# Layer norms of a two-layer trunk: sums over channels and their factors taken as whole tiles

## The chip, the cores and the metric

The kernel runs on one core of a Trainium2 chip. Times are device microseconds of one execution. A row of the profile has times in microseconds from the start of the profiled execution, and names a line of the kernel as L followed by its number. The engines are TensorE (PE; its weight loads are PEld), VectorE (DVE), ScalarE (ACT), GpSimd (POOL) and SyncE (SP), which issues most transfers.

## The reference

The input x has 1024 tokens with 1024 channels, in float32. Each layer computes x = x + mixer(rmsnorm(x)), and a last rmsnorm follows:

```python
def rmsnorm(x, g):
    xf = x.astype(jnp.float32)
    y = xf * lax.rsqrt(jnp.mean(xf * xf, axis=-1, keepdims=True) + EPS)
    return (y * g.astype(jnp.float32)).astype(x.dtype)
```

Layer 0 projects h to six parts (u, a gate, q, k, v, a second gate). u goes through a diagonal state-space recurrence and a GLU, q, k and v through retention in chunks of 64 tokens; each result is multiplied by its SiLU gate, and one product maps both back to 1024 channels. Layer 1 projects to a, b and g, convolves a * sigmoid(b) over 31 tokens per channel, norms the result over the channels with mean and variance, and applies SiLU, the gate and an output product:

```python
    mu = jnp.mean(uf, axis=-1, keepdims=True)
    var = jnp.mean(jnp.square(uf - mu), axis=-1, keepdims=True)
    uf = (uf - mu) * lax.rsqrt(var + EPS) * ln_g.astype(jnp.float32) + ln_b.astype(jnp.float32)
```

So there are four norms, each with a factor per token that is the inverse root of a mean over all channels.

## The kernel before

Activations lie with channels on the 128 partitions and tokens along the free dimension, so that a 1024 x 1024 activation is eight channel blocks of 128 x 1024, handled as two halves of 512 tokens. A product of 1024 channels with one 128-column weight block is 24 matmuls of 128 x 128 by 512: the operands are split into a high and a low part in the format fp32r, and each of the eight channel blocks takes three products, high by high, high by low and low by high (`mm3`, L181 to L183). SP streams the weight blocks of 512 KB from HBM through three buffers; ACT makes the high part (L171) and DVE or POOL the low part (L172). Products gather in PSUM banks: three for running products (`mm`), five for other uses in the front, two kinds for the convolution later.

Nobody writes the order of the instructions by hand. A scheduler places each instruction on its engine's queue as its operands allow, by a priority that `self.at(number)` sets (lower goes first), and `issue_after(x)` forbids an instruction to be placed ahead of x. What two instructions share on one engine they do in the queue's order: a waiting instruction holds those behind it.

A norm before the change goes in these steps. The squares of the eight channel blocks are added up to one tile, on ACT with DVE or POOL. `token_sums` (L444) sums that tile over the partitions: for each 128 tokens the data is the stationary operand and 64 columns of ones the moving one, so that the sum of a token lands on the token's own partition. `rsqrt` (L453, L454) then works on 4 or 8 values per partition: a square root on ACT and a reciprocal on DVE. To multiply the channel-major tiles, the factor must be on all partitions along the free dimension: `spread_split` makes diagonal tiles, the identity times the factor, a high and a low one, and multiplies ones by them (L473); `spread` (L483) does it with one f32 product per 256 columns.

The places are these.

- `layer0_front`: the tile R0 (`self.R`, all partitions, 1024 tokens) and `Rtok` (the same factors, tokens on partitions, which the retention's v blocks use). The first products are u blocks 0 and 1 for both halves; then u2 (the half 0 in one piece, half 1 in eight steps of three products), with the token sums behind step 0 and the spreads before step 5; ACT copies the spread factors from PSUM to R (L335). Then DVE evacuates the blocks: `u_block(nb)` multiplies the block's two PSUM banks by R into a tile `ut` (L356), which has two buffers, and SP stores that tile to `u_d`. Blocks 0, 1 and 2 are evacuated from banks that were filled before R; block 3 and later ones compute into a running bank, half by half, so that they need a bank which an earlier evacuation has freed. On DVE's queue beside the evacuations are steps on the parameters of the recurrence (lines L531 to L549) and low parts of weights.
- `h1(h)`, the norm ahead of layer 1, one factor for each half (r1). The eight blocks are then scaled by it (L1374) and split into high and low parts for the products b, g and a.
- `conv_norm(h)`, with two sums (values and squares), the variance and the factor on 4 values per partition, and two spreads: the factor (cR) and the mean times the factor (cD).
- `final_norm`: half 0 as a whole, half 1 in two quarters of 256 tokens. The last quarter ends the kernel; it keeps PE running with a few products that nobody reads (`idle`) and spreads twice, one copy for ACT (`rf_C`).

The products around a norm have `hold` lists: at which step of which block the product must stay behind the sums or spreads of the norm (`self.hold`, `among`, `norm_mm`), and one list of convolution steps on DVE that must stay behind a norm's diagonals (`NORM_TAPS`).

## Time and profile before

| | |
|---|---|
| median of 3 runs | 1183.63 us (1182.59 to 1185.37) |
| profiled execution | 1188.26 us, span 1186.5 us |
| PE | 1173.5 us busy, 99 % |
| PE weight loads | 985.8 us, 83 % |
| DVE | 851.1 us, 72 % |
| POOL | 657.4 us, 55 % |
| ACT | 483.6 us, 41 % |
| mean granted clock of PE | 0.995 of full speed |
| HBM traffic | 216 GB/s over the span |

The span is the time between the first and the last instruction of the profiled execution. A row of the timeline gives start and busy time, engine, line, operation, output<-inputs, the shape (for a matmul the stationary tile and then the moving one), and how many like instructions it joins; a bracket at the end gives the idle time before it and who ended it. A row of the waits gives an engine's instruction, the one that it waited for, the total of the waits, their number and the longest. A row of the windows gives the stretch, its length, the busy time and instructions of PE, PEld, DVE, ACT and POOL, the granted clock, the share of the DMA engines and GB/s.

### The profile page before, as it was taken

How to read it: one execution, taken by the hardware profiler on the slowest of the kernel's cores; microseconds unless marked ns; L12 is line 12 of the kernel's file. 1: busy time of each engine (PE TensorE's matmuls, PEld its weight loads, DVE VectorE, ACT ScalarE, POOL GpSimd, SP SyncE). 2: the span in 40 equal slices, each digit the busy share in tenths (PEclk: the TensorE clock that was granted, in tenths of full speed). 3: DMA queues.
4: the chain of work that ended last, by engine and by line, in shares of the span. 5: the costliest groups of instructions: out<-in, count | busy, mean ns of one | idle time of the engine just before them, and what ended most of it. 6: DMA issues, size and time to landing. Idle time of an engine off the chain costs nothing.

```text
span 1186.5 us, 17318 instructions
## 1 busy us (share of the span) xinstructions
PE 1173.5 (99%) x6326; PEld 985.8 (83%) x6326; DVE 851.1 (72%) x1479; ACT 483.6 (41%) x712; POOL 657.4 (55%) x448
## 2 busy tenths in 40 slices
PE   9999999999999999899999999999999999999997
PEld 7888888888888889889888888888888888888886
DVE  7975698777427458476679422699999999989743
ACT  6322232222222231333546322545435676434662
POOL 2059999888145354232574110678444567767753
PEclk9999999999999999999999999999999999999999
DMA  9344355565387676759998987655668754357874
GB/s 355 107 129 136 131 156 167 182 186 170 109 280 280 233 231 181 259 177 343 371 344 290 336 266 254 213 198 196 227 243 280 231 180 166 107 189 253 268 246 145
DMA packets 117637, 261.46 MB, mean 220 GB/s; under 512 B 10672, under 2 KB 42288, under 8 KB 116912
## 3 DMA queue, kind: packets, MB, share of 16 engines
q1 hardware_dynamic: 117552, 260.36, 65.4%
q8 instruction: 49, 0.80, 0.3%
q14 instruction: 36, 0.29, 0.1%
HBM read 181.48 MB, written 74.65 MB: 216 GB/s over the span
## 4 chain that ended last, share of the span: by engine, by line
PE 93%; DMA 3%; DVE 2%; issue 1%; SPq 0%; POOL 0%; ACT 0%; POOLq 0%; DVEq 0%; ACTq 0%
PE mm_g L181 8%; PE mm_g L183 7%; PE mm_g L182 7%; PE mm_wo L182 5%; PE mm_wo L181 5%; PE mm_wo L183 5%; PE mm_b L182 2%; PE mm_b L183 2%; PE mm_a L183 2%; PE mm_a L182 2%; PE mm_b L181 2%; PE mm_a L181 2%; PE mm_oc L181 2%; PE mm_oc L183 2%; PE mm_oc L182 2%; PE mm_u L183 2%
## 5 line engine op out<-in xcount | busy, mean ns | idle before, releaser
L1467 DVE SCALAR_TENSOR_TENSOR cv<-u,convw,cv 128x512 f32<-128x512 f32 x398 | 273.7, 751 | 9.0 <-ACT cv L1450 6.9
L1444 POOL TENSOR_TENSOR tp<-tp,tp 128x512 f32<-128x512 f32 x64 | 83.7, 1307 | 35.2 <-ACT tp L1443 34.0
L181 PE MATMUL mm_g<-xh,wh_g 128*128 128x512 f32 x256 | 101.8, 398 | 0.0
L183 PE MATMUL mm_g<-xh,wl_g 128*128 128x512 f32 x256 | 100.1, 391 | 0.0
L182 PE MATMUL mm_g<-xl,wh_g 128*128 128x512 f32 x256 | 100.0, 391 | 0.0
L415 POOL TENSOR_TENSOR s1q<-s1q,s1q 128x512 f32<-128x512 f32 x12 | 17.7, 1478 | 85.2 <-ACT s1q L410 85.2
L1443 ACT ACTIVATE tp<-u,convw 128x512 f32<-128x512 f32 x64 | 45.6, 719 | 37.3 <-POOL tp L1444 35.8
L181 PEld LDWEIGHTS mm_g<-xh,wh_g 128*128 128x128 f32 x256 | 48.0, 188 | 11.7 <-issue 1.2
L183 PEld LDWEIGHTS mm_g<-xh,wl_g 128*128 128x128 f32 x256 | 48.1, 188 | 10.4
L182 PEld LDWEIGHTS mm_g<-xl,wh_g 128*128 128x128 f32 x256 | 48.1, 188 | 9.9 <-issue 0.4
L371 DVE TENSOR_TENSOR gt<-mm_g,R 128x512 f32<-128x512 f32 x32 | 21.9, 684 | 46.5 <-PE mm_g L183 46.4
L172 POOL TENSOR_TENSOR wl_glu<-wf_glu,wh_glu 128x1024 fp32r<-128x1024 f32 x14 | 34.0, 2428 | 33.8 <-ACT wh_glu L171 33.2
L183 PE MATMUL mm_oc<-zh,wl_woc 128*128 128x512 f32 (+1 forms) x144 | 52.5, 366 | 0.0
L172 POOL TENSOR_TENSOR wl_v<-wf_v,wh_v 128x1024 fp32r<-128x1024 f32 x12 | 31.1, 2601 | 38.5 <-ACT wh_v L171 38.5
L182 PE MATMUL mm_oc<-zl,wh_woc 128*128 128x512 f32 (+1 forms) x144 | 52.5, 366 | 0.0
L181 PE MATMUL mm_oc<-zh,wh_woc 128*128 128x512 f32 (+1 forms) x144 | 52.3, 369 | 0.0
L181 PE MATMUL mm_g<-h1h,wh_cg 128*128 128x512 f32 x128 | 49.9, 390 | 0.0
L181 PE MATMUL mm_wo<-ysh,wh_wos 128*128 128x512 f32 x128 | 49.9, 390 | 0.0
L182 PE MATMUL mm_b<-h1l,wh_cb 128*128 128x512 f32 x128 | 49.9, 390 | 0.0
L183 PE MATMUL mm_g<-h1h,wl_cg 128*128 128x512 f32 x128 | 49.8, 389 | 0.0
L181 PE MATMUL mm_b<-h1h,wh_cb 128*128 128x512 f32 x128 | 49.8, 389 | 0.0
L182 PE MATMUL mm_a<-h1l,wh_ca 128*128 128x512 f32 x128 | 49.8, 389 | 0.0
(506 smaller groups left out, 3663.6 us busy)
## 6 DMA issues: line engine op xcount, KB each, us to landing
wf_g<-w_ab SPq DMA_DIRECT2D x16, 512.0 KB
wf_wos<-w_out SPq DMA_DIRECT2D x16, 512.0 KB
wf_wor<-w_out SPq DMA_DIRECT2D x16, 512.0 KB
wf_cb<-w_c SPq DMA_DIRECT2D x16, 512.0 KB
wf_ca<-w_c SPq DMA_DIRECT2D x16, 512.0 KB
wf_woc<-w_out_c SPq DMA_DIRECT2D x16, 512.0 KB
wf_v<-w_v SPq DMA_DIRECT2D x12, 512.0 KB
wf_cg<-w_c SPq DMA_DIRECT2D x11, 512.0 KB
```

Source lines behind the costliest of these rows:

```text
L172: self.low_made = lo[i].tensor_tensor(wl[:].rearrange(fl)[:, c], wf[:, c], h.bitcast(F32), op=ALU.subtract)
L181: nc.tensor.matmul(ps, wh[:, kb, :], xh, start=start, stop=False, **more)
L182: nc.tensor.matmul(ps, wh[:, kb, :], xl, start=False, stop=False, **more)
L183: self.last_mm = nc.tensor.matmul(ps, wl[:, kb, :], xh, start=False, stop=stop, **more)
L371: nc.vector.tensor_tensor(gt[:, c], ps[:], self.R[:, c], op=ALU.mult)
L415: nc.gpsimd.tensor_tensor(a, a, sq[:], op=ALU.add)
L1443: nc.scalar.mul(sk[:], u[:, k:k + HALF], cw[:, nb, k:k + 1])
L1444: gp.tensor_tensor(s0[:], s0[:], sk[:], op=ALU.add)
L1467: v.scalar_tensor_tensor(dst[:], *tap, accs_[i][:], op0=ALU.mult, op1=ALU.add)
```

## The change

A sum is now one matmul per 512 tokens with a 128 x 128 tile of ones stationary and the data moving, in plain f32 (`wide_sums`): every partition gets the sum of every token, so no spread follows. The factor is computed on that whole tile (`wide_rsqrt`): ACT takes the logarithm of sum times scale plus epsilon, the exponential of minus one half of it, and a scaled square of that; DVE does one Newton step for the inverse root with two instructions and writes the factor. Ahead of them ACT loads the table that holds logarithm and exponential (`table`), behind the last square.

In the front the sums of the two halves stand behind steps 0 and 1 of u2's second half, and each half's factor is written straight into R. `Rtok` is got from R by way of HBM: SP stores one row of R to `r_d` and loads it again with tokens on partitions. In `conv_norm` the mean's square, the variance and the product of mean and factor are whole tiles too. `final_norm` uses the wide form for half 0 and the first quarter; the last quarter keeps the narrow form (`rstd_last`), and loads the table of the square root ahead of it. The hold lists keep only the sums. The helper tile `mhalf` is gone.

```diff
@@ -214,14 +213,13 @@
...
         self.u_d = dt("u_d", [8, 8, 16, 8, P])
         self.y_d = dt("y_d", [8, 8, 16, 8, P])
+        self.r_d = dt("r_d", [1, T])
...
@@ -319,26 +317,21 @@
 
         self.R = self.mid.tile([P, T], F32, name="R0")
         self.Rtok = self.mid.tile([P, 8], F32, name="Rtok")
-        rps = acc[1]
 
         w_u2 = self.wnext("u2")
         u2 = [self.bank(f"mm_u2_{h}", aux=False) for h in range(2)]
         self.gemm(u2[0][:], w_u2, xs[0])
-        u2_step = lambda kb: self.mm3(u2[1][:], w_u2, kb, (xs[1][kb][0][:], xs[1][kb][1][:]), kb == 0, kb == KB - 1)
-        u2_step(0)
-        with self.tc.issue_after(self.last_mm.ins):
-            self.token_sums([(rps, ssum[:])])
-        self.rsqrt(self.Rtok[:], rps[:].rearrange("p (b x) -> p b x", x=64)[:, :, 0], 1.0 / D)
-        for h in range(2):
-            rp = acc[h]
-            self.spread_split(rp[:], self.Rtok[:, 4 * h:4 * h + 4], ev, f"r0_{h}", (("dg", 2), ("sq", 2)), True)
-            nc.scalar.copy(self.R[:, h * HALF:(h + 1) * HALF], rp[:])
-
-
-        r_diag = self.last_diag
-        for kb in range(1, KB):
-            with self.tc.issue_after(self.last_spread.ins) if kb >= RMM else nullcontext():
-                u2_step(kb)
+        for kb in range(KB):
+            self.mm3(u2[1][:], w_u2, kb, (xs[1][kb][0][:], xs[1][kb][1][:]), kb == 0, kb == KB - 1)
+            if kb < 2:
+                c = slice(kb * HALF, (kb + 1) * HALF)
+                with self.tc.issue_after(self.last_mm.ins):
+                    self.wide_sums(acc[kb][:], [ssum[:, c]])
+                self.wide_rsqrt(acc[kb][:], ev, f"r0_{kb}", 1.0 / D, self.R[:, c], bufs=2)
+        r_ready = self.last_newton
+
+        nc.sync.dma_start(self.r_d[:], self.R[0:1, :])
+        nc.sync.dma_start(self.Rtok[:], self.r_d[0].rearrange("(b p) -> p b", p=P))
 
         def scaled(nb, w, name, cb):
             for h in range(2):
@@ -376,7 +369,7 @@
 
         for nb in range(3):
             u_block(nb)
-        with self.tc.issue_after(xdma.ins), self.tc.issue_after(r_diag.ins):
+        with self.tc.issue_after(xdma.ins), self.tc.issue_after(r_ready.ins):
             zero = ev.tile([P, P], F32, name="zero")
             nc.gpsimd.memset(zero[:], 0.0)
             nc.sync.dma_start(self.k_d[:, :112].rearrange("b r c -> r b c"),
@@ -436,78 +429,72 @@
             self.tc.cur_priority = old
         return cm()
 
-    def token_sums(self, terms):
-
-        terms = [(ps[:, b * 64:(b + 1) * 64], a[:, b * P:(b + 1) * P]) for ps, a in terms
-                 for b in range(a.shape[1] // P)]
-        for i, (o, a) in enumerate(terms):
-            self.last_stat = self.nc.tensor.matmul(o, a, self.ones[:, :64], start=i == 0, stop=i == len(terms) - 1)
-
-    def rsqrt(self, dst, src, scale=1.0, pool=False):
+    def wide_sums(self, ps, parts):
+
+        for i, a in enumerate(parts):
+            self.last_stat = self.nc.tensor.matmul(ps, self.ones[:], a, start=i == 0, stop=i == len(parts) - 1)
+
+    def wide_rsqrt(self, src, pool, name, scale=1.0, dst=None, copy=None, bufs=1, table=True):
+
+
+        nc, v, n = self.nc, self.nc.vector, src.shape[1]
+        half = pool.tile([P, HALF], F32, name=f"{name}_ha", tag="sq", bufs=bufs)[:, :n]
+        y = copy
+        if y is None:
+            y = pool.tile([P, HALF], F32, name=f"{name}_y", tag="dg", bufs=bufs)[:, :n]
+        dst = src if dst is None else dst
+        after = self.squared
+        if table:
+            with self.tc.issue_after(after.ins):
+                after = nc.scalar.preload_act_table_set("natural_log_exp_and_others")
+        with self.tc.issue_after(after.ins):
+            nc.scalar.activation(y, src, AF.Ln, scale=scale, bias=self.epst[:])
+        nc.scalar.activation(y, y, AF.Exp, scale=-0.5)
+        self.halved = nc.scalar.activation(half, y, AF.Square, scale=(0.5 * scale) ** 0.5)
+        v.scalar_tensor_tensor(src, src, EPS / scale, half, op0=ALU.add, op1=ALU.mult)
+        self.last_newton = v.scalar_tensor_tensor(dst, src, 1.5, y, op0=ALU.subtract, op1=ALU.mult, reverse0=True)
+        if copy is not None:
+            nc.scalar.copy(copy, dst)
+
+    def rsqrt(self, dst, src, scale=1.0):
 
         nc = self.nc
-        if pool:
-            nc.vector.tensor_scalar(dst, src, scale, EPS, op0=ALU.mult, op1=ALU.add)
-            nc.gpsimd.tensor_tensor(dst, dst, self.mhalf[:, :dst.shape[1]], op=ALU.pow)
-        else:
-            root = nc.scalar.activation(dst, src, AF.Sqrt, scale=scale, bias=self.epst[:])
-            nc.vector.reciprocal(dst, dst)
-            return root
-
...
-    def rstd(self, parts, pool, name, idle=0):
+        root = nc.scalar.activation(dst, src, AF.Sqrt, scale=scale, bias=self.epst[:])
+        nc.vector.reciprocal(dst, dst)
+        return root
+
+    def rstd(self, parts, pool, name, copy=None, table=True):
+
+        n = parts[0].shape[1]
+        ps = self.bank(f"{name}_R")
+        self.wide_sums(ps[:, :n], parts)
+        self.wide_rsqrt(ps[:, :n], pool, name, 1.0 / D, copy=copy, table=table)
+        return ps
+
+    def rstd_last(self, parts, pool, name):
 
         nc = self.nc
         n = parts[0].shape[1]
         nb = n // P
...
+        with self.tc.issue_after(self.halved.ins):
+            nc.scalar.preload_act_table_set("sqrt_and_others")
+
+        ps, wait, *rp = (self.bank(f"{name}_{k}", aux=False) for k in ("ps", "wait", "R", "C"))
+        terms = [(b, a[:, b * P:(b + 1) * P]) for a in parts for b in range(nb)]
+        for i, (b, a) in enumerate(terms):
+            last = nc.tensor.matmul(ps[:, b * 64:(b + 1) * 64], a, self.ones[:, :64], start=i == 0, stop=i == len(terms) - 1)
+
+        with self.tc.issue_after(last.ins):
+            for _ in range(IDLE):
+                last = nc.tensor.matmul(wait[:, :P], self.ones[:], self.ones[:], start=True, stop=True)
         r4 = pool.tile([P, 4], F32, name=f"{name}_r4", tag="r4", bufs=2)[:, :nb]
         self.rsqrt(r4, ps[:, 0:64 * nb].rearrange("p (b x) -> p b x", x=64)[:, :, 0], 1.0 / D)
...
+        dg = pool.tile([P, 4, P], F32, name=f"{name}_dg", tag="sq", bufs=1)[:, :nb, :]
+        nc.vector.tensor_tensor(dg, self.ident[:].unsqueeze(1).broadcast_to([P, nb, P]),
+                                r4.unsqueeze(2).broadcast_to([P, nb, P]), op=ALU.mult)
+        with self.tc.issue_after(last.ins):
+            for o in rp:
+                nc.tensor.matmul(o[:, :n], self.ones[:], dg.rearrange("p b t -> p (b t)"), start=True, stop=True)
         return rp
 
 
@@ -1511,30 +1498,23 @@
 
         def conv_norm(h):
             sm, acc = accs[("cv", h)]
-            st = ps_cv.tile([P, HALF], F32, name=f"cst_{h}", tag="cn")
+            s1, s2 = (ps_cv.tile([P, HALF], F32, name=f"cst{i}_{h}", tag="cn") for i in range(2))
             q7 = csquare(h, 7)
-            s1, s2 = st[:, 0:256], st[:, 256:512]
 
             e = v if h else gp
             e.tensor_tensor(sm[:], sm[:], cv[h][7][:], op=ALU.add)
             e.tensor_tensor(acc[:], acc[:], q7[:], op=ALU.add)
-            self.token_sums([(s1, sm[:]), (s2, acc[:])])
-            st4 = st[:].rearrange("p (k b x) -> p k b x", k=2, x=64)
-
-            t4 = [lp.tile([P, 4], F32, name=f"cn4_{i}_{h}", tag=f"cn4_{i}", bufs=1) for i in range(4)]
-            d4, q4, v4, r4 = (t[:] for t in t4)
-            nc.scalar.activation(q4, st4[:, 0, :, 0], AF.Square, scale=1.0 / D)
-            nc.scalar.mul(d4, st4[:, 0, :, 0], 1.0 / D)
-            v.scalar_tensor_tensor(v4, st4[:, 1, :, 0], 1.0 / D, q4, op0=ALU.mult, op1=ALU.subtract)
-            self.rsqrt(r4, v4)
-            v.tensor_tensor(d4, d4, r4, op=ALU.mult)
-            Rp = ps_cv.tile([P, HALF], F32, name=f"cR_{h}", tag="cn")
-            self.spread_split(Rp[:], r4, lp, f"cR_{h}")
-            Dp = ps_cv.tile([P, HALF], F32, name=f"cD_{h}", tag="cn")
-            with self.tc.issue_after(self.last_diag.ins):
-                self.spread_split(Dp[:], d4, lp, f"cD_{h}", (("tp", 3),) * 2 if h else (("dg", 1), ("sq", 1)))
-            self.norm_mm[h] = self.last_stat, self.last_spread
+            self.wide_sums(s1[:], [sm[:]])
+            first = self.last_stat
+            self.wide_sums(s2[:], [acc[:]])
+            self.norm_mm[h] = first, self.last_stat
+
+            m2 = lp.tile([P, HALF], F32, name=f"cm2_{h}", tag="dg", bufs=1)
+            self.squared = nc.scalar.activation(m2[:], s1[:], AF.Square, scale=1.0 / D)
+            v.scalar_tensor_tensor(s2[:], s2[:], 1.0 / D, m2[:], op0=ALU.mult, op1=ALU.subtract)
             R = lp.tile([P, HALF], F32, name=f"RL_{h}", tag="cq", bufs=1)
+            self.wide_rsqrt(s2[:], lp, f"cn_{h}", copy=R[:], table=bool(h))
+            Rp = s2
             dl = lp.tile([P, HALF], F32, name=f"dl_{h}", tag="cs", bufs=1)
             for nb in range(8):
                 c = cv[h][nb]
@@ -1543,8 +1523,7 @@
                 z = ps_cv.tile([P, HALF], F32, name=f"zz{nb}_{h}", tag="cv") if e is v else c
                 e1.tensor_tensor(z[:], c[:], (R if e1 is gp else Rp)[:], op=ALU.mult)
                 if nb == 0:
-                    nc.scalar.copy(R[:], Rp[:])
-                    nc.scalar.copy(dl[:], Dp[:])
+                    v.scalar_tensor_tensor(dl[:], s1[:], 1.0 / D, R[:], op0=ALU.mult, op1=ALU.mult)
                 e.tensor_tensor(z[:], z[:], dl[:], op=ALU.subtract)
                 nc.scalar.activation(z[:], z[:], AF.Silu, scale=self.vec(V_LNG, nb), bias=self.vec(V_LNB, nb))
                 tag, bufs = ("ld", 2) if h == 0 else ("tp", 3) if nb < 3 else ("u", 5)
@@ -1591,13 +1570,15 @@
             n = c.stop - c.start
             end = h and c.stop == HALF
             R = lp.tile([P, HALF], F32, name=f"RF_{h}_{c.start}", tag="dg", bufs=1)
-            rp = self.rstd([final[h][nb][1][:, c] for nb in ((0, KB - 1) if end else (0,))], lp, f"rf_{h}_{c.start}",
-                           IDLE if end else 0)
+            if end:
+                rp, copied = self.rstd_last([final[h][nb][1][:, c] for nb in (0, KB - 1)], lp, f"rf_{h}_{c.start}")
+            else:
+                rp = self.rstd([final[h][0][1][:, c]], lp, f"rf_{h}_{c.start}", R[:, :n], h == 0)
             for nb in (4, 5, 0, 1, 2, 3, 6, 7) if end else range(8):
                 if nb == 4:
                     yield
-                if nb == (4 if end else 1):
-                    nc.scalar.copy(R[:, :n], (self.copied if end else rp)[:, :n])
+                if end and nb == 4:
+                    nc.scalar.copy(R[:, :n], copied[:, :n])
                 t = final[h][nb][0]
                 e = gp if (nb // 2 == 2 if end else nb % 3 == 2) else v
                 c0 = h * HALF + c.start
@@ -1615,17 +1596,16 @@
         with self.at(100000):
             w_out(0, range(8))
             h1(0)
-        self.hold = {4: self.last_stat, 8: self.last_spread}
+        self.hold = {4: self.last_stat}
         with self.at(200000):
             w_out(1, range(2))
             with self.at(110000):
                 ab(0)
             w_out(1, range(2, 8))
             h1(1)
-        self.norm_first = self.last_sum, self.last_diag
+        self.norm_first = self.last_sum
         with self.at(300000):
-            gates((0,), range(G0), {0: {4: self.last_stat, 7: self.last_spread}, 1: {0: self.last_spread},
-                                  2: {0: self.last_spread}})
+            gates((0,), range(G0), {0: {4: self.last_stat}, 1: {0: self.last_stat}, 2: {0: self.last_stat}})
             with self.at(210000), self.tc.issue_after(self.last_mm.ins):
                 ab(1)
             gates((0, 1), range(G0, 8))
```

In the lines not shown, `NORM_TAPS` becomes `NORM_TAP = 23, 11` (one hold, behind the norm's last sum of squares on the adding engine, for the convolution steps), the hold of the first blocks of half 1 in layer 1 names the two sums of `conv_norm` instead of a sum and a spread, the quarters' list `among` names the sums alone, and three places keep the last square as `self.squared`.

More of the change, by code (lines that the diff above doesn't have):

```diff
@@ L30 @@
 WARM = 14
-RMM = 5
 IDLE = 4
@@ L476, in spread @@
-    def spread(self, ps, r4, pool, name, tag="dg", bufs=1, more=()):
-        nb = r4.shape[1]
-        dg = pool.tile([P, 4, P], F32, name=f"{name}_dg", tag=tag, bufs=bufs)[:, :nb, :]
-        self.last_diag = self.nc.vector.tensor_tensor(
-            dg, self.ident[:].unsqueeze(1).broadcast_to([P, nb, P]), r4.unsqueeze(2).broadcast_to([P, nb, P]), op=ALU.mult)
-        for o in (ps, *more):
-            self.last_spread = self.nc.tensor.matmul(o, self.ones[:], dg.rearrange("p b t -> p (b t)"), start=True, stop=True)
@@ L1465, in conv @@
                         continue
-                    with self.tc.issue_after(ahead[-1].ins) if ahead else nullcontext():
+                    with self.tc.issue_after(self.norm_first.ins) if ahead else nullcontext():
                         v.scalar_tensor_tensor(dst[:], *tap, accs_[i][:], op0=ALU.mult, op1=ALU.add)
@@ L1657, in layer0_back_and_layer1 @@
                     continue
-                stat, spread = self.norm_mm[1]
-                blocks(0, range(N0, 8), {N0: {HOLD: stat}, N0 + 1: {0: spread}})
+                first, stat = self.norm_mm[1]
+                blocks(0, range(N0, 8), {N0: {HOLD: stat}, N0 + 1: {0: stat}})
             with self.at(410000):
```

49 lines of the change are left out of this document (7 added, 42 removed).

## Prediction

> **What bounds the kernel now.** I read the page first, then TensorE's waits, then the chain that ended last.
>
> ```profile
> span 1186.5 us, 17318 instructions
> PE 1173.5 (99%) x6326; PEld 985.8 (83%) x6326; DVE 851.1 (72%) x1479; ACT 483.6 (41%) x712; POOL 657.4 (55%) x448
> ...
> PE 93%; DMA 3%; DVE 2%; issue 1%; SPq 0%; POOL 0%; ACT 0%; POOLq 0%; DVEq 0%; ACTq 0%
> ```
>
> TensorE (PE) sets the time: it is busy for 99% of the span. What the change takes from its queue is won unless a wait takes its place. Its waits are few:
>
> ```profile
> PE sp L1133 <- DVE S L1126: 3.5, 1, 3.5
> ...
> PE mm_u L181 <- DVE ut L356: 0.3, 1, 0.3
> ```
>
> The second is small but sits at the end of a chain without slack, the only one in the front part of the kernel. The chain that ended last (start, length, work):
>
> ```profile
> 40.37 0.59 ACT R L335
> 40.99 2.17 DVE ut L356 x2
> 43.26 1.05 DVE ut L356
> 44.33 3.09 DMA u_d<-ut
> 47.44 1.13 DVE ut L356
> 48.71 0.47 PE mm_u L181
> ```
>
> Read it so: the first norm's factor R is ready; DVE evacuates both halves of blocks u0 and u1; block 0's tile is stored (3.09 us); only then may block 2 use that tile buffer; its first half is evacuated and frees the PSUM bank in which the second half of u3 starts at 48.71. Whatever makes this chain later delays PE one for one.
>
> **PE work removed.** Rows of the timeline (start, busy):
>
> ```profile
> 730.99 1.00 PE L444 MATMUL r_ps<-ones,s1q 128*128 128x64 f32 x8
> 731.79 0.48 PE L181 MATMUL mm_wo<-ysh,wh_wos 128*128 128x512 f32 x1
> ...
> 738.05 0.39 PE L473 MATMUL r_R<-r_dg,ones_r 128*128 128x512 f32 x1
> 738.28 0.40 PE L183 MATMUL mm_wo<-ysh,wl_wos 128*128 128x512 f32 x1
> ...
> 1110.20 1.00 PE L444 MATMUL cst<-ones,cs 128*128 128x64 f32 x8
> 1111.90 0.48 PE L181 MATMUL mm_oc<-zh,wh_woc 128*128 128x512 f32 x1
> ...
> 1116.80 0.62 PE L473 MATMUL cR<-cR_dg,ones_r 128*128 128x512 f32 x2
> 1118.34 0.39 PE L181 MATMUL mm_oc<-zh,wh_woc 128*128 128x512 f32 x1
> ...
> 1178.87 0.70 PE L483 MATMUL rf_R<-rf_dg,ones 128*128 128x256 f32 x2
> 1179.40 0.59 PE L483 MATMUL rf_C<-rf_dg,ones 128*128 128x256 f32 x2
> ```
>
> Start to start, four token sums take 0.80 us, a spread product 0.23, the eight sums of the conv norm 1.70, and that norm's four spreads 1.54 in the second half. A wide sum (ones by a whole 512-column f32 tile, two passes) is not in the trace. The same form with 256 columns takes 0.53; twice that is 1.06, the upper end, and two ordinary 0.23 products the lower, 0.46. I take 0.9, because the 0.53 follows a standstill, and the first product after a change of kind shows some 0.1 more than the next (731.79 holds 0.48 instead of 0.39).
>
> - r1, both halves: 0.80 + 2 x 0.23 - 0.9 = 0.36 each, together 0.7.
> - Conv norm, first half, with spreads between other work: 1.70 + 4 x 0.23 - 1.8 = 0.8. Second half: 1.70 + 1.54 - 1.8 = 1.4.
> - Final norm of half 0: 0.4.
>
> Sum 3.3 us saved outside the front and the last quarters. Between 0.46 and 1.06 per wide sum it is 5.9 to 2.3. It counts in full because PE has no wait in these stages that could absorb it.
>
> **The front (R0).** These rows carry the new chain:
>
> ```profile
> 34.72 1.22 DVE L172 TENSOR_TENSOR wl_u<-wf_u,wh_u 128x1024 fp32r<-128x1024 f32 x1
> 34.88 1.28 ACT L453 ACT_TABLE_LOAD   x1 [0.46 <-DVE ssum L268]
> 34.89 1.96 PE L444 MATMUL ss<-ones,ssum 128*128 128x64 f32 x16
> ...
> 38.99 0.42 DVE L549 TENSOR_SCALAR s_s_ci<-s_s_ci 128x512 f32<-128x512 f32 x1
> ...
> 40.26 0.14 DVE L531 TENSOR_SCALAR s5t<-s5t 128x32 f32<-128x32 f32 x1
> 40.37 1.15 ACT L335 COPY R<-ss 128x512 f32<-128x512 f32 x2
> ...
> 40.73 0.39 PE L181 MATMUL mm_u<-xh,wh_u 128*128 128x512 f32 x1
> ...
> 47.53 0.39 PE L181 MATMUL mm_u<-xh,wh_u 128*128 128x512 f32 x1
> ```
>
> PE first. Thirty products lie between 40.73 and 47.53, so 0.227 each. Two wide sums, the 21 products left of u2 and the 24 of u3's first half: 34.89 + 1.8 + 45 x 0.227 = 46.9. There PE wants the bank that block 2 must free; before, it began there at 48.71.
>
> Now the factor, with two groups of instructions (line, engine, operation, count, busy us, mean ns):
>
> ```profile
> L1467 DVE SCALAR_TENSOR_TENSOR cv<-u,convw,cv 128x512 f32<-128x512 f32 x398 | 273.7, 751 | 9.0 <-ACT cv L1450 6.9
> ...
> L1581 ACT ACTIVATE s2q<-x 128x512 f32<-128x512 f32 x14 | 8.7, 628 | 4.8 <-DVE x L1580 4.8
> ```
>
> First sum complete at 35.9. ACT has by then loaded its table (1.28, now ahead of the cast) and cast. Ln, Exp and Square on 512 columns are not in the trace at this place; the copy from PSUM (0.58) is the lower and the squares of L1581 (0.63) the upper end; with the hand-over of dependent work 0.65 each: 37.9. Two DVE steps at 0.75 (the L1467 row): R's first half at 39.5, 1.5 us earlier than the first evacuation began before.
>
> But DVE's queue in the changed kernel then reads: two evacuations (2.1), the second half's two steps (1.5), which wait for nothing any more, the parameter steps that before filled the time while R was made (38.99 to 40.26, so 1.3) and the low part of u5's weights (1.1 to 1.2). 39.5 + 2.1 + 1.5 + 1.3 + 1.2 = 45.6. Block 0's second half then ends at 46.6, against 44.3 before. So the first half's gain is spent by work that stood beside the old chain and now stands in it. Storing block 0 takes the chain's 3.1 again, hence 49.8; fourteen small steps like the one at 40.26 (0.14 and the hand-over) keep DVE to about 50 anyway.
>
> SP's queue: the new store of R's row and the new load of Rtok (1,024 values of 4 bytes, 128 x 8) stand ahead of the store of block 0, and with them wf_g. The load waits for the store on SP; everything behind it waits too. R is whole at 43.1; one round trip of about 2 to 3 us (3.09 is the only row near) and the issues free SP at about 46.4, just in time. The bytes of wf_g (0.5 MB, which came after block 0's store before) and Rtok's pieces now pass first: 0 to 3.1, the price of a whole store of as many pieces. I take 0.9, nearer zero, because nothing else is in flight then. So block 2's evacuation starts at 50.7, PE at 51.9: 3.2 later than 48.71 and after a wait of 5.0 instead of 0.3. Both ends: 49.5 (no transfer in front, shorter ACT steps) and 54.
>
> **What a 5 us wait does to PE.** The other long wait shows it. Same products before it and after it, and the clock after it:
>
> ```profile
> 406.40 1.04 PE L1133 MATMUL sp<-qrot,krot 64*128 64x128 f32 x13
> ...
> 410.14 1.16 PE L1160 MATMUL ro<-S,qrot 64*128 64x128 f32 x16
> ...
> 503.25 1.83 PE L1133 MATMUL sp<-qrot,krot 64*128 64x128 f32 x13 [3.49 <-DVE S L1126]
> ...
> 509.92 0.38 PE L1160 MATMUL ro<-S,qrot 64*128 64x128 f32 x2
> ```
> ```profile
> 503.00:508.00 5.00, 4.75 (x32) 4.53 (x33) 4.86 (x11) 0.00 (x0) 1.27 (x1) 0.50 0.00 0
> ```
>
> A stretch of scores and outputs that took 410.14 - 406.40 = 3.74 us took 509.92 - 503.25 = 6.67 after 3.49 us of idleness, at a granted clock of 0.50: 2.9 us more. The front's wait is longer, so I charge 2.9 there too; ends 0 (the 0.3 us waits cost nothing) and 3.4 (twice over).
>
> The Trainium skill, "TensorE: Matmul & The Clock Gate", Part 1, says that the gate closes after an idle window of about 3.4 us and that this window runs free, so its phase varies from run to run. By that rule the same 5 us wait halves the clock in some runs and not in others; this trace's 0.50 agrees with the halving, and no run here shows the phase. By the rule the change would cost 2.9 in some runs and 0.0 in the others.
>
> **Costed at nothing.** r1, half 0: the factor comes about 3 us earlier (731.9 + 0.65 x 3 + 1.5 = 735.4, where the first scaling began at 738.95), and the scheduler has moved h1's first product up to 55 products behind the sum, 731.9 + 55 x 0.227 = 744.4:
>
> ```profile
> 738.95 1.29 DVE L1374 TENSOR_TENSOR xn<-x1n,r_R 128x512 f32<-128x512 f32 x2 [4.84 <-PE r_R L473]
> ...
> 749.64 0.39 PE L181 MATMUL mm_b<-h1h,wh_cb 128*128 128x512 f32 x1
> ```
>
> That leaves 9 us where there were 10.7. If the cover is gone, up to 1. r1, half 1: eight scalings of h1 now stand behind four convolution steps (0.75) on DVE instead of two; three gate blocks, 72 products or 16 us, cover them; without cover 2. Conv norms: per norm DVE loses four diagonals and eight steps on a few values and gains four steps of 0.75; ACT's Ln, Exp, Square stand in idle time (41% busy), and the second half's factor comes no later by 1112.0 + 1.3 + 3 x 0.65 + 1.5 = 1116.8 than the spreads that began at 1116.80. Last quarters: quarter 0 saves PE some 0.2, but Ln, Exp, Square and a table load of 1.28 now stand ahead of the last square on ACT, and six products ahead of the last reciprocal on DVE: it comes 6.2 us after quarter 0's sum, where the rows give 1178.12 - 1171.98 = 6.1:
>
> ```profile
> 1171.98 0.56 PE L444 MATMUL rf_ps<-ones,s2q 128*128 128x64 f32 x4
> ...
> 1178.12 0.17 DVE L454 RECIPROCAL rf_r<-rf_r 128x2 f32<-128x2 f32 x1 [0.50 <-ACT rf_r L453]
> ```
>
> So +0.1.
>
> **Sum:** -3.3 + 3.2 + 0.1 + 2.9 = +2.9 on a profiled execution of 1188.26 (its span and 1.8 around it). That run lies 4.6 above the median 1183.63; I carry the difference over: 1183.6 + 2.9 = 1186.5.
>
> **Rivals.**
> - The clock stays up through the wait: +0.0, 1183.6. For it: 5.0 is not much over 3.49. Against it: the only long wait of the trace closed it.
> - Faster: the second factor and block 0's second half come early enough, so that PE does not stand still and the clock holds. The first evacuation's 1.5 us speaks for it; DVE's order speaks against it. It decides where u3's second half starts before 49.5; at 49 the sum is -3.3 + 0.3 + 0.1, 1180.7.
> - The gather of Rtok holds block 0's store for the whole 3.1 instead of 0.9: PE starts at 54.1, 1188.7. For it: it has as many pieces as that store. The Trainium skill, "DMA: Bandwidth & Descriptors", Rules for kernel authors, says that a strided last dimension becomes one descriptor per element; by that rule this is the case to expect, and no row here has such a load.
> - The wide sum is no cheaper than four sums and two spreads (1.26 instead of 0.9): six outside, two in the front, 3.0 more, 1189.5. The 256-column row speaks against it.
>
> **How the numbers follow.** Forecast 0.47 (own range 1184.8 to 1188), clock stays up 0.20, faster 0.11, Rtok 0.15, wide sums and the rest 0.07. The range 1180.7 to 1189.8 leaves out about 2 in 10: half of the faster case, and the top of the forecast and of the last two. 0.2% (2.4 us) is about what a measurement tells from no change. Faster: the faster case and a little of the second, 0.15. Same: most of the second and the lower edge of the forecast, 0.29. Slower: 0.56.
>
> **What would show it.** After: PE waits 4 to 6 us for DVE ut near 47 us, and the granted clock is 0.50 for some 6 us behind it; the chain there runs through u_d<-ut again; wide sums start 0.9 apart from what follows; PE's other gaps stay as they are. Wrong if u3's second half starts before 49.5, if PE waits over 1 us anywhere new after 60 us, or if the wide sums cost over 1.1.

## The result

The changed kernel took 1189.97 us (median of 6 runs, 1189.23 to 1192.3) where the kernel before took 1183.66 (1182.59 to 1186.1): a ratio of 1.0052, 95% interval 1.0038 to 1.0065. The change makes the kernel 6.3 us slower. Forecast were 2.9 us, 1186.5, with a range up to 1189.8. The direction was right, the size was not. The profiled execution took 1192.3 us, with a span of 1190.5.

First the page of the changed kernel, then TensorE's waits (who waited, for whom: total, number, longest):

```profile
PE 1169.7 (98%) x6250; PEld 978.2 (82%) x6250; DVE 851.0 (71%) x1452; ACT 492.6 (41%) x716; POOL 655.2 (55%) x448
```
```profile
PE mm_u L180 <- DVE ut L349: 5.2, 1, 5.2
PE cst L435 <- DVE cs L1505: 3.9, 1, 3.9
PE sp L1120 <- DVE S L1113: 1.5, 1, 1.5
...
PE rf_R L497 <- DVE rf_dg L493: 0.7, 1, 0.7
PE rf_ps L485 <- ACT s2q L1560: 0.6, 1, 0.6
PE cst L435 <- DVE cq L1506: 0.6, 1, 0.6
```

PE is busy for 3.8 us less than before, and the span is 4.0 longer. Two waits of some length are new. The 5.2 us for `ut` is the front's, as forecast. The 3.9 and 0.6 us for `cs` and `cq`, the operands of the sums in the convolution's norm, half 1, were not in the forecast. A third new one, 0.7 us for `rf_dg` in the last quarter, is small.

The front came out nearly as worked out. The chain that ended last there (start, length, work):

```profile
35.26 0.87 PE ss L435 x2
...
39.67 2.18 DVE ut L349 x2
41.85 0.62 DVE ss L454
...
44.45 1.11 DVE wl_u L171
45.55 1.05 DVE ut L349
...
46.62 4.50 DMA u_d<-ut
```

Block 0's second half ends at 46.6 (worked out: 46.6), its store takes 4.50 instead of 3.09 (worked out: 0.9 more), and u3's second half starts at 52.35 (worked out: 51.9). The clock behind it:

```profile
50.00:57.50 7.50, 5.15 (x13) 4.12 (x14) 6.61 (x35) 0.00 (x0) 0.00 (x0) 0.54 0.55 160
```

To say where the time went, another trace of the kernel before is a better yardstick than the one that the prediction was made from (why stands at e12 below): one of 1183.57 us, span 1181.5, near the median. The same points of both programs, PE's row there, first the kernel before in that trace (e12), then the changed kernel:

```profile
48.78 0.47 PE L181 MATMUL mm_u<-xh,wh_u 128*128 128x512 f32 x1 [0.35 <-DVE ut L356]
...
395.41 0.60 PE L1097 MATMUL ktp<-ident,krot 128*128 128x128 f32 x4
...
726.04 1.00 PE L444 MATMUL r_ps<-ones,s1q 128*128 128x64 f32 x8
...
901.35 1.00 PE L444 MATMUL r_ps<-ones,s1q 128*128 128x64 f32 x8
...
942.54 1.00 PE L444 MATMUL cst<-ones,cs 128*128 128x64 f32 x8
...
1105.25 1.00 PE L444 MATMUL cst<-ones,cs 128*128 128x64 f32 x8
...
1140.64 1.00 PE L444 MATMUL rf_ps<-ones,s2q 128*128 128x64 f32 x8
```
```profile
52.35 0.77 PE L180 MATMUL mm_u<-xh,wh_u 128*128 128x512 f32 x1 [5.15 <-DVE ut L349]
...
401.74 0.60 PE L1084 MATMUL ktp<-ident,krot 128*128 128x128 f32 x4
...
733.11 1.02 PE L435 MATMUL r_R<-s1q,ones 128*128 128x512 f32 x2
...
907.91 1.02 PE L435 MATMUL r_R<-s1q,ones 128*128 128x512 f32 x2
...
948.71 1.02 PE L435 MATMUL cst<-cs,ones 128*128 128x512 f32 x2
...
1114.18 1.12 PE L435 MATMUL cst<-cs,ones 128*128 128x512 f32 x2 [3.93 <-DVE cs L1505]
...
1150.25 1.02 PE L435 MATMUL rf_R<-s2q,ones 128*128 128x512 f32 x2
```

| point | behind before, us | what the step holds |
|---|---|---|
| u3, second half | +3.6 | the front's wait |
| first retention products | +6.3 | +2.8: mostly the half clock behind that wait |
| sums of r1, half 0 | +7.1 | +0.7: retention |
| sums of r1, half 1 | +6.6 | -0.5: r1 saves products |
| conv norm, half 0 | +6.2 | -0.4: r1 again |
| conv norm, half 1 | +8.9 | +2.8: the wait of 3.9, less 1.2 saved |
| final norm, half 0 | +9.6 | +0.7: 0.6 more wait and half clock, less what is saved |
| end of the span | +9.0 | -0.6 |

The spans of these two executions differ by 9.0 us. The profiled one of the changed kernel lies 2.3 above its own median; that rest of its spread is not explained.

### The profile page after: what moved, and what is told of

It reads as the page before. It is cut to its first block, busy times and chain, and to the rows that moved or that the text cites. A ratio compares the mean times of both kernels' runs of the same rounds, so it can differ in the third digit from the quotient of the medians.

```text
span 1190.5 us, 17134 instructions
## 1 busy us (share of the span) xinstructions
PE 1169.7 (98%) x6250; PEld 978.2 (82%) x6250; DVE 851.0 (71%) x1452; ACT 492.6 (41%) x716; POOL 655.2 (55%) x448
## 2 busy tenths in 40 slices
DMA packets 118679, 261.47 MB, mean 220 GB/s; under 512 B 11713, under 2 KB 43329, under 8 KB 117954
## 4 chain that ended last, share of the span: by engine, by line
PE 93%; DVE 3%; issue 2%; DMA 1%; ACT 1%; POOL 0%; POOLq 0%; SPq 0%; DVEq 0%; ACTq 0%
PE mm_g L180 7%; PE mm_g L181 7%; PE mm_g L182 7%; PE mm_wo L182 5%; PE mm_wo L180 5%; PE mm_wo L181 5%; PE mm_b L182 2%; PE mm_a L182 2%; PE mm_a L180 2%; PE mm_b L180 2%; PE mm_a L181 2%; PE mm_b L181 2%; PE mm_oc L181 2%; PE mm_oc L182 2%; PE mm_oc L180 2%; PE mm_u L180 2%
## 5 line engine op out<-in xcount | busy, mean ns | idle before, releaser
L180 PE MATMUL mm_u<-xh,wh_u 128*128 128x512 f32 x128 | 50.3, 405 | 5.2 <-DVE ut L349 5.2
L182 PE MATMUL mm_b<-h1h,wl_cb 128*128 128x512 f32 x128 | 50.6, 395 | 0.0
L181 PE MATMUL mm_u<-xl,wh_u 128*128 128x512 f32 x128 | 50.4, 398 | 0.0
```

The source lines that it names most:

```text
L180: nc.tensor.matmul(ps, wh[:, kb, :], xh, start=start, stop=False, **more)
L181: nc.tensor.matmul(ps, wh[:, kb, :], xl, start=False, stop=False, **more)
L182: self.last_mm = nc.tensor.matmul(ps, wl[:, kb, :], xh, start=False, stop=stop, **more)
```

## The experiments

Each group was timed beside the kernel before on the same chip; a ratio is that of the experiment to the kernel before, with its 95% interval. The interval is 0.2 to 0.3% to either side, so a single edit of 2 us is seen in its trace and hardly in its time.

**Which part costs it: e1 and e2.** e1 puts the new R0 front into the kernel before (the second hunk of the diff, `wide_sums`, `wide_rsqrt` and `r_d`). e2 puts the front of before into the changed kernel.

> The kernel before with the front's part of the change alone (wide sums, factor on whole tiles, Rtok by way of HBM). Theory A, the front costs what its trace shows: PE waits 5.2 us for ut_2 and loses some 2.7 us more at half clock, so u3's second half starts near 52.4 and the time is 6 us above before, near 1189.7. Theory B, lateness in the front is given back in the retention, whose wait for S was 3.5 us before and 1.5 after: 2 us above before, near 1185.7.

> The changed kernel with the front of before. Theory A: no wait near 47 us, 6 us below the changed kernel, near 1184. Theory B: 2 us below it, near 1188, and the wait of the convolution's sums alone carries the loss.

Measured: e1 1190.75, 1.0052 (1.0032 to 1.0071); e2 1189.99, 1.0034 (1.0014 to 1.0055). e1 is as theory A has it: the front alone costs about 6 us, its trace has the wait of 5.3. e2 is as neither has it: without the front the changed kernel is still some 4 us slower, with the 3.9 us wait for `cs` in its trace. So there are two losses, and if the savings of 3.3 came in full, the second is as large as these and 4 more. The two measured parts, 6 and 4 us, are together more than the change's 6.3. Each is known to some 2.3 us only; whether the rest is noise, or lateness that is made up in other waits, no run separates.

**The front: e3 and e11.** e3 gives block u2 a tile of its own:

```diff
-            ut = uv.tile([P, 8, P], F32, name=f"ut_{nb}", tag="ut", bufs=2)
+            ut = (ev.tile([P, 8, P], F32, name="ut_2", tag="ut2") if nb == 2 else
+                  uv.tile([P, 8, P], F32, name=f"ut_{nb}", tag="ut", bufs=2))
```

To make room, the logarithm's output is written into R's own slice, and the Newton step multiplies it in place.

> The changed kernel with a third tile for block u2 in the front (its own buffer), so that the evacuation of u2 no longer waits for the store of block 0; all else as in the change, Rtok's way included. If the chain through that store makes the front's loss: no wait of PE for ut over 1 us before 60 us, the clock stays at 1.0, and the time is 6 to 8 us below the changed kernel, 1182 to 1184. If the wide factor itself is too late, or Rtok's transfers hold SP: the wait stays at 2 us or more, 1187 to 1190.

Measured: 1187.5, 1.0009 (0.9988 to 1.003), against 1.0052 for the change, so some 5 us better where 6 to 8 were expected. The trace is the first case's: the wait for `ut` is gone and the clock is 1.0 from 34 to 100 us. In the trace of e10, which has the same front, DVE evacuates the first halves of three blocks in a row as soon as R's first half is there:

```profile
39.65 3.25 DVE L350 TENSOR_TENSOR ut<-mm_u,R 128x512 f32<-128x512 f32 x3
```

So the factor is not late, and Rtok's way by HBM, still ahead of the stores, costs PE nothing there once no evacuation hangs on a store. The loss was the buffer: the third evacuation waits for block 0's second half and its store.

e11 leaves the wait and fills it with twenty products of ones into a free bank.

> The changed kernel with twenty products of ones that nobody reads, on PE ahead of u3's second half, so that PE is busy for most of the wait of 5.2 us there. The wait for ut keeps its end near 52.4. If the half clock behind that wait costs 2.7 us: the clock stays at 1.0 from 34 to 100 us and the time is 2 to 3 us below the changed kernel, 1187 to 1188. If PE is late for other work anyway and the loss is given back: no change, 1189 to 1191.

Measured: 1196.27, 1.0088 (1.0058 to 1.0118): slower than the change. The edit did not leave the rest as it was: the store of block 0 took 6.47 us in this trace, for a reason that is not shown, and u3's second half came later (x40: each product counts twice):

```profile
47.52 4.62 PE L345 MATMUL ss<-ones 128*128 128x128 f32 x40
54.78 0.47 PE L181 MATMUL mm_u<-xh,wh_u 128*128 128x512 f32 x1 [2.63 <-DVE ut L355]
```

A wait of 2.6 us is left, and the clock is 0.50 for a time behind it. It says nothing clean of the price of the half clock.

**The wait for the sums: what makes `cs` late.** The rows of DVE in the kernel before, then DVE and POOL in the changed kernel:

```profile
1106.45 0.70 DVE L1460 TENSOR_TENSOR cv<-cv,pilot 128x512 f32<-128x512 f32 x1
1107.18 0.75 DVE L1467 SCALAR_TENSOR_TENSOR co<-u,convw,cv 128x512 f32<-128x512 f32 x1
1108.04 1.39 DVE L1519 TENSOR_TENSOR cs<-cs,co 128x512 f32<-128x512 f32 x1
1109.35 0.68 DVE L1520 TENSOR_TENSOR cq<-cq,cvq 128x512 f32<-128x512 f32 x1
1110.40 0.69 DVE L1580 TENSOR_TENSOR x<-mm_oc,x1l 128x512 f32<-128x512 f32 x1 [0.37 <-PE mm_oc L183]
```
```profile
1108.73 0.70 DVE L1447 TENSOR_TENSOR cv<-cv,pilot 128x512 f32<-128x512 f32 x1
1110.29 0.69 DVE L1559 TENSOR_TENSOR x<-mm_oc,x1l 128x512 f32<-128x512 f32 x1 [0.86 <-PE mm_oc L182]
1110.90 0.74 DVE L1454 SCALAR_TENSOR_TENSOR co<-u,convw,cv 128x512 f32<-128x512 f32 x1
1111.74 2.38 DVE L1505 TENSOR_TENSOR cs<-cs,co 128x512 f32<-128x512 f32 x1
1114.05 1.75 DVE L1506 TENSOR_TENSOR cq<-cq,cvq 128x512 f32<-128x512 f32 x1
...
1111.23 2.35 POOL L171 TENSOR_TENSOR wl_woc<-wf_woc,wh_woc 128x1024 fp32r<-128x1024 f32 x1 [1.19 <-ACT wh_woc L170]
1113.54 1.71 POOL L1564 TENSOR_TENSOR s2q<-s2q,s2q 128x512 f32<-128x512 f32 x1
```

Before, PE comes to the sums of `cs` at 1110.20, and to those of `cq` here:

```profile
1111.03 1.06 PE L444 MATMUL cst<-ones,cq 128*128 128x64 f32 x8
```

The addition for `cs` ends at 1108.04 + 1.39 = 1109.43 and that for `cq` at 1110.03: 0.8 and 1.0 us of slack, on a chain that DVE sets. After, PE comes to the sums at 1114.18 - 3.93 = 1110.25, and three things differ. The evacuation of the fifth output block (`x<-mm_oc`) stands ahead of the last convolution step, and it waits for the last product ahead of the sums: DVE waits for PE, and then PE for DVE. With the wait of 0.86 it costs DVE 1.5 us. And the additions, which take 0.7 us elsewhere, take 2.4 and 1.8: each ends some 0.5 us behind the POOL step beside it. That costs 1.7 ahead of the first sum. The same is in the row of before, 1.39, beside this row of POOL:

```profile
1107.58 1.29 POOL L1585 TENSOR_TENSOR s2q<-s2q,s2q 128x512 f32<-128x512 f32 x1
```

Third, DVE is further back in its convolution ahead of these two: the step `cv<-cv,pilot` began 3.75 us before PE came to the sums (1106.45, 1110.20) and begins 1.52 before it now (1108.73, 1110.25). That leaves 0.8 of the 3.9 us, the wait that stays in e9 and e16 below. What brings this part, PE's saved products, DVE's own waits or the order, no run separates; with r1 of before (e7) the lead is 2.95. The convolution steps, which read one operand from PSUM, keep their 0.75 us under POOL's steps (the L1467 row of the prediction). The Trainium skill, "SBUF — State Buffer", section "SBUF: two separate sides", says that a DVE instruction with two SBUF inputs and a GpSimd instruction that reads SBUF exclude each other for a whole instruction, whoever is first; both additions of the changed kernel agree with it.

e4 gives PE more work ahead of the sums (`N0, HOLD = 6, 1`).

> The changed kernel with six blocks of the output product ahead of the sums of the convolution's norm in half 1 instead of five (N0 = 6): 5.4 us more of other work on PE ahead of the wait of 3.9 and 0.6 us. If that wait lies on the path: both waits go, 4 to 4.5 us below the changed kernel, near 1185.5. If what follows the norm (its factor and the scaled blocks) sets the end anyway, a wait of the same length appears behind the last of the six blocks: no gain, near 1190.

Measured: 1191.19, 1.0045 (1.0026 to 1.0065). The rival held in substance: the waits for the sums are gone, and 3.8 us stand behind the eighth block instead, at the first products of half 1, for the scaled blocks that the norm's factor makes.

```profile
PE mm_oc L180 <- ACT zh L1185: 3.8, 2, 2.6
```

So the place to gain is on DVE, ahead of the sums, not on PE. e6 and e7 ask which part of the change brought DVE's order.

> The changed kernel with the convolution's norm of before (sums of 64 columns, variance and factor on 4 values, two spreads); the front, r1 and the final norm stay wide. If the whole-tile steps of that norm (its two table loads on ACT and DVE's waits for ACT near 950 us) make DVE late at the second half's sums: the wait of 3.9 us goes or falls below 2, 3 to 5 us below the changed kernel, 1185 to 1187. If the order that r1's steps give to DVE's queue makes it: the wait stays at 3 to 4 us, and the time rises by the sums that cost more, 1190 to 1192.

> The changed kernel with r1 of before (both halves); the front, the convolution's norm and the final norm stay wide. DVE's queue then has the evacuation of the fifth output block behind the two additions again. If r1's steps make the convolution late: the wait for the sums falls from 4.5 us to below 2, and the time by 2 to 4 us, 1186 to 1188. If the convolution's norm makes it: the wait stays at 3 us or more, 1189 to 1191.

e6 puts `conv_norm` of before into the changed kernel: 1194.74, 1.0074 (1.0045 to 1.0103), and the wait of 3.9 us stays to the tenth, with the evacuation at the same place. The whole-tile steps of that norm are not the cause. e7 puts `token_sums`, `rsqrt` and `spread_split` back for r1 alone: the evacuation stands behind the additions again, and PE waits nowhere for `cs`. So r1's form decides the order that the scheduler gives to DVE some 200 us later. The time did not follow, 1193.46, 1.0058 (1.0038 to 1.0077): 3.5 us of other waits came in r1's stage (2.0 for `h1l`, 1.5 for `sgg`), where buffers and order differ too. e7 settles the cause of the order, not its price.

e8 was a first mend with several edits at once, the fifth block traced later, POOL's weight steps told to stay behind the additions, the third tile and one table load less.

> The changed kernel with four edits: the third tile for u2 in the front; the fifth output block's evacuation behind the two additions ahead of the convolution's sums; POOL's low parts of the weights of blocks 6 and 7 behind them too; and one table load for logarithm and exponential in the first half's norm instead of two. If the two waits (front 5.2, sums 4.5) and the half clock behind them are the whole loss: both are below 1 us, the two additions take 0.7 us each instead of 2.4 and 1.8, and the time is 8 to 12 us below the changed kernel, 1178 to 1182. If the lateness only moves on, to the factor or the scaled blocks of that norm: PE waits 2 to 4 us there and the time stays above 1183.

Measured: 1188.91, 1.0019 (0.9997 to 1.0041), and a wait of 3.9 us for `cs` again. The edit moved PE's blocks as well, so that another evacuation, the fourth block's, took the same place; and the hold did not move POOL's step, since it orders instructions within one engine's queue alone. It tells nothing of the cause.

e9 moves the one instruction and nothing else: the evacuation of the fifth block is traced behind the additions.

```diff
+                if (h, nb) == (0, N0 - 1):
+                    self.fifth = finish
+                else:
+                    finish()
...
+            adds = e.tensor_tensor(acc[:], acc[:], q7[:], op=ALU.add)
+            if h:
+                with self.at(400000), self.tc.issue_after(adds.ins):
+                    self.fifth()
```

> The changed kernel with one instruction moved on DVE: the evacuation of the fifth output block stands behind the two additions ahead of the convolution's sums instead of ahead of the last convolution step. PE's order, POOL's and all work are the same. If that place makes the wait of 3.9 us (the evacuation waits for PE's last product, and the last step and the additions stand behind it): the additions come 1.5 us earlier and miss POOL's weight step, the wait is below 1 us, the second one (0.6) goes, and the time is 4 to 6 us below the changed kernel, 1184 to 1186. If DVE is late there in any case: the wait is 2 to 3 us and the time 1 to 2 us below.

Measured: 1192.15, 1.0064 (1.004 to 1.0088); the time shows no gain. The trace does, in part: the waits are 0.8 for `cs` and 2.0 for `cq` instead of 3.9 and 0.6. DVE and POOL:

```profile
1109.87 0.69 DVE L1505 TENSOR_TENSOR cs<-cs,co 128x512 f32<-128x512 f32 x1
1111.34 2.33 DVE L1506 TENSOR_TENSOR cq<-cq,cvq 128x512 f32<-128x512 f32 x1 [0.78 <-ACT cvq L1473]
...
1110.79 2.34 POOL L171 TENSOR_TENSOR wl_woc<-wf_woc,wh_woc 128x1024 fp32r<-128x1024 f32 x1 [1.19 <-ACT wh_woc L170]
```

The first addition escapes POOL's step and takes 0.69. The second waits 0.8 for ACT's square, by which time POOL's step has begun, and takes 2.33. Both come from one ACT instruction, the cast of the eighth block's weights: it stands ahead of the square, and POOL's step follows it. e16 tests that.

**Both mended: e10, e15, e16.** e10 is e3 and e9 together, e15 adds `HOLD = 5`, and e16 is e10 with that cast held behind the square:

```diff
-            nc.scalar.copy(h, wf[:, c])
+            with self.tc.issue_after(self.csq.ins) if name == "woc7_0" else nullcontext():
+                nc.scalar.copy(h, wf[:, c])
```

> Both edits together, the third tile in the front and the evacuation behind the additions. If the two waits and the half clock behind them are what the change loses: neither is over 1 us, and the time lies 2 to 4 us below the kernel before, 3.3 us by the products saved. If not: at or above it, and a new wait of PE shows where.

> The third tile in the front and the evacuation behind the additions, and the sums of half 1 behind five steps of the sixth output block instead of one (HOLD = 5, twelve products or 2.7 us more ahead of the wait). If the waits are the loss: no wait for the sums over 1 us, and 4 to 6 us below the kernel before, 1178 to 1180. If the norm's factor then comes too late for the scaled blocks: a wait of mm_oc for zh or zl of 2 us or more, and no gain over the version with the two edits (0.9987 of before).

> The kernel of e10 (third tile in the front, evacuation behind the additions) with one ACT instruction moved: the cast of the eighth output block's weights stands behind the square that the second addition needs, so the square comes 1 us earlier and POOL's low part of these weights, which follows the cast, starts after both additions. If ACT's order and POOL's step make the rest of the wait: the second addition takes 0.7 us instead of 2.3, the two waits for the sums are 0.8 and below 0.3 us, the clock behind them stays at 1.0, and the time is 2 to 4 us below e10's, 0.995 to 0.998 of before. If the low part now comes late for its block or the additions are slow in any case: a wait of mm_oc for wl_woc, or 2 us left for the sums, and no gain over e10.

Measured: e10 1183.44, 0.9987 (0.9966 to 1.0007), with the 0.8 and 2.0 us of e9 still in its trace; e15 1184.03, 0.9995 (0.9976 to 1.0013), with new waits for `zh` and `zl` (2.2 and 0.9), as its second case has it; e16 1184.25 beside 1185.57, 0.9982 (0.9965 to 1.0000). In e16 the additions (DVE) and POOL's step behind them:

```profile
1103.52 0.69 DVE L1507 TENSOR_TENSOR cs<-cs,co 128x512 f32<-128x512 f32 x1
1104.18 0.69 DVE L1508 TENSOR_TENSOR cq<-cq,cvq 128x512 f32<-128x512 f32 x1
...
1105.09 2.38 POOL L172 TENSOR_TENSOR wl_woc<-wf_woc,wh_woc 128x1024 fp32r<-128x1024 f32 x1 [1.85 <-ACT wh_woc L171]
```
```profile
PE cst L437 <- DVE cs L1507: 0.8, 1, 0.8
```

Both additions take 0.69, one wait of 0.8 is left, and the clock stays at 1.0 there. That shows the two parts of the wait. Their price in time is less sure: e16 is no faster than e10 by more than the noise (0.9982 and 0.9987), where 2 to 4 us were expected, and against e3, which has the whole wait, it gains 3 us with intervals that overlap. What is clear of noise is both losses together: 1.0052 for the change, 0.9982 with both mended, some 8 us. The mended change is about 2 us faster than the kernel before, at the edge of what these runs can tell.

**The yardstick: e5, e12, e13, e14.** The kernel before once more, three times for a trace, and the changed kernel beside it.

> The kernel before, once more, for a second trace of it. If its time goes with the granted clock (1183.8 at 0.999 and 1190.6 at 0.995 in the runs so far) and the clock with the wait in the retention: a time near 1183.8 has 0.998 or 0.999, the wait for S below 3.5 us or no half clock behind it; a time near 1188 has both again. If the spread has another source, the wait and the half clock stand there in either case.

> The kernel before, a third trace. If executions without the half clock in the retention exist (0.998 or 0.999, near 1183.8): in such a trace the wait for S is below 2 us and the clock stays at 1.0 from 500 to 520 us. If this one is near 1188 again, it has both.

> The kernel before, a fourth trace, for the same question: near 1183.8 without the half clock in the retention, or near 1188 with it.

> The changed kernel beside the kernel before on this chip: 5 to 7 us slower, with the waits of 5.2 us for ut and 4.5 us for the sums, the retention's wait shorter than before's.

Measured: e5 1188.74, e12 1183.57, e13 1184.31; e14 1191.59, 1.0054 (1.0033 to 1.0075), with both waits, but with 2.5 us and half clock in the retention, so in this trace its wait for S is not shorter than before's, which had been expected. The wait for S in the retention and the stretch from 500 to 520 us, e5 and then e12:

```profile
PE sp L1133 <- DVE S L1126: 2.0, 1, 2.0
```
```profile
500.00:520.00 20.00, 17.60 (x107) 15.27 (x106) 18.37 (x65) 2.24 (x5) 3.65 (x3) 0.83 0.37 130
```
```profile
PE sp L1133 <- DVE S L1126: 0.8, 1, 0.8
```
```profile
500.00:520.00 20.00, 19.30 (x131) 16.76 (x132) 19.23 (x68) 4.52 (x7) 6.50 (x5) 1.00 0.50 159
```

The half clock in the retention is in some executions and not in others, and the time goes with it: the two traces of the kernel before that have it took 1188.3 and 1188.7 us, the two without it 1183.6 and 1184.3. In the 35 runs of the kernel before beside e1 to e4, by granted clock over the span:

| clock | runs | mean, us |
|---|---|---|
| 0.999 | 16 | 1183.8 |
| 0.998 | 6 | 1184.2 |
| 0.997 | 6 | 1187.4 |
| 0.996 | 4 | 1189.2 |
| 0.995 | 3 | 1190.6 |

The profiled execution behind the prediction had 0.995: it was one of the rarer ones.

## Why the prediction was wrong

Right, by its own steps: PE bound; the wide sum at 0.9 (0.87 in the chain above, so the case that it is no cheaper fell); the front's chain through `u_d<-ut`, PE at 51.9 (52.35) after a wait of 5.0 (5.2); the wait's 3.2 and the clock's 2.9 together 6.1 (e1 alone 6.2; 2.8 for the clock in the table above); Rtok's transfers ahead of the store at 0.9 (the store took 1.4 more, not 3.1, though the gather did go in single values: 11713 packets under 512 B where there were 10672); r1 0.36 each (0.5 and 0.4). The cases that the clock stays up, that the front starts before 49.5 and that Rtok holds the store for 3.1 did not come. On the clock rule that the prediction named, by which the same wait would halve the clock in some runs and not in others: in the front every trace with a wait of 5 us had the half clock behind it (after, e1, e4, e6, e7, e9, e14), so no run bears that case out for a wait of this length. What did vary is how long it lasted: 6.8 us in five of these traces (50.5 to 57.3 in the profiled one) and 3.4 in e4 and e6 (52.4 to 55.8 in e4). Half of the part behind the wait is the price, so 1.6 to 2.9 us, and 2.5 in the profiled execution.

Wrong: the sentence that the savings count in full because PE has no wait in these stages that could absorb it, and with it the cover named for the convolution's norms. It looked at where PE waited before, and at the time from the sums to the factor, but never at who has the sums' operands ready, and when: DVE, 0.8 us ahead of PE for the first of them, which is less than the 1.5 that the evacuation alone takes there now. What came there is the wait of 3.9 and 0.6 us and half clock behind it. By the table the part from the conv norm's half 0 to the final norm cost +3.4 (8.9 - 6.2 and 9.6 - 8.9), where the forecast had -1.4 for half 1 and -0.8 for half 0: 5.6 us. With the 2.9 forecast that is 8.5, against 9.0 between the two traces and 6.3 between the medians. That the medians are 2.7 nearer stays open; 2.3 of it is the profiled execution's place above its median.

The list of signs held this one: wrong if PE waits over 1 us anywhere new after 60 us. The order of DVE's queue, with the evacuation ahead of the last step, could be read from the program before it ran; it was read for the front, r1 and the last quarter, not there.

The baseline was a second fault, smaller: the sum was made against an execution with 3.5 us of wait and half clock in the retention, and carried to the median as a plain shift. For the front and the savings that was harmless, as the agreement with e12 shows.

## What to carry to other kernels

Where one engine is 99% busy, a saving on it is safe only if the other engine that feeds each join has slack there: take the end of the last operand and the start of the consumer from the trace, at every join that the change moves, not only where a wait is shown. An evacuation that waits for the main engine must not stand in a queue ahead of the operands that this engine needs next. And an edit of the instructions in one stage can reorder a scheduled queue much later, so read the order there too.

## What the runs showed that was not expected

- The half clock came behind waits shorter than the prediction weighed: 1.8 us (e1) and 2.0 (e5) in the retention and 2.6 (e11) in the front, while 0.8 (e12) and, in e13 and the changed kernel, 1.5 in the retention left it at 1.0. But 2.6 us in e4 (1129.9 to 1132.5) and 1.9 in e16 (ahead of 183.2) left it at 1.0 too, so the length alone does not decide. The Trainium skill, "TensorE: Matmul & The Clock Gate", Part 1, names an idle window of about 3.4 us; here some 2 us of standstill were enough in some traces and not in others.
- Two f32 additions on DVE went from 0.7 to 2.4 and 1.8 us beside POOL steps, which makes a POOL step that nobody waits for part of PE's chain.
- The store of block 0 (0.5 MB), 3.09 us before, took 4.50 with Rtok's gather of 4 KB and the load of wf_g ahead of it.
